# One cast and one subtraction of 2048 columns for the four sums of weights of a seven-product chunk, instead of two of each of 1024

## The chip, the core and the metric

One of the eight cores of a Trainium2 chip runs the kernel. The metric is device time in microseconds (us): the median of three runs. Each core has five engines that run their own instruction streams and wait for each other by semaphores: TensorE (PE in the profile, its weight loads PEld), VectorE (DVE), ScalarE (ACT), GpSimd (POOL) and SyncE (SP, which issues the DMAs here).

## What is computed

A decoder layer on 256 tokens of width 2048, all in float32:

```python
h = h + 0.5 * swiglu(rmsnorm(h, g_ffn1), w1_gate, w1_up, w1_down)   # D_FF = 5632
z = rmsnorm(h, g_mix) @ w_in
...                                                                # gating group A, windowed attention group B
h = h + y @ w_out
h = h + cross_attention(rmsnorm(h, g_x), rmsnorm(mem, g_mem), w_xq, w_xkv, w_xo)
h = h + 0.5 * swiglu(rmsnorm(h, g_ffn2), w2_gate, w2_up, w2_down)
return rmsnorm(h, g_final)
```

with `swiglu(x, wg, wu, wd) = (silu(x @ wg) * (x @ wu)) @ wd`. Almost all of the time goes into products of 256 rows with large weight matrices; the two SwiGLUs hold most of them.

## The kernel before

**Split products.** PE multiplies in the type fp32r. So that the result is good to float32, each operand is split into a high part (a cast, on ACT) and a low part (operand minus high part, on DVE), and each product is made in three passes: high by high, low activations by high weights, high activations by low weights. `split` does this: its cast is L146, its subtraction L147.

**Chunks and units.** The weights come in chunks of 1 MB (128 x 4 x 512). Eight chunks make a unit in the gate and up products (`gu_unit`; 11 units in each SwiGLU, named f1g and f2g in the profile); the down projections (f1d, f2d) have 44 chunks each, in four units. A chunk multiplies 2 x 2 blocks of activations by 2 x 2 blocks of weights in one of three ways: as eight plain products (N, C; 24 matmuls) or in a seven-product scheme (S; 21 matmuls). In an S chunk the seven products need sums of weight blocks, T1, T3, T2, T4 in this order: `load` (L304) adds them up into the tile t with three additions on DVE (L319 of 1024 columns, L322 and L323 of 512), splits three of the four raw blocks into wh and wl (1536 columns, L324), and then splits the four sums: two of them into one pair of tiles (th0, tl0), two into another (th1, tl1), in the loop at L326. In N and C chunks the four raw blocks are split at once into wh and wl (2048 columns). Units 2 to 9 of a gate and up product have kinds SCSCSCSC, units 0, 1 and 10 CCSCSCSC (unit 0 of the first SwiGLU is plain). 137 chunks are S chunks: 38 in f1g, 41 in f2g, 16 in f1d, 16 in f2d, 26 in the layer's middle.

**Buffers.** Raw weights have three buffers, wh and wl two each, t, th and tl one each. So the split of chunk n+2 into wh waits until PE is done with chunk n, and a th tile is written again only when PE has used the last one.

**Order on PE.** PE's order is written by hand. Matmuls are issued in `Unit.run` at L410. In the first and the last chunk of a unit the low weights of a product come right behind its high weights (`by_bank` in `passes`); in the chunks between, the low weights tl of the four sums come at the chunk's end (the list `behind`). Between matmuls, PE makes transposes of finished activations (L230, in `rows_done`, two groups for each unit, during chunk 2 of the next unit). Such a group needs a free bank of a ring of four in PSUM, which the unit's late products share; the second group gets its bank only when ACT has copied the first out (L665).

**Order on the other engines.** The instructions on DVE, ACT and SP are put in an order at build time by a scheduler with an idea of its own about how long each takes. On the chip, each engine runs its list strictly in that order. At the end of a unit the seven products are put together: `seven_early` behind the last S chunk (L560 to L562: p1, v and z), `seven_late` behind chunk 7 (L567 to L571), and then `gated` (an activation at L671, products at L675).

Of the kernel before, what the change touches and what calls it, by code (L numbers as in the profile page):

```python
# [9 lines left out]
F32R = mybir.dt.float32r  # L10
# [4 lines left out]
P = 128  # L15
# [17 lines left out]
def layer_kernel(  # L33
# [26 lines left out]
    stream = ctx.enter_context(tc.tile_pool(name="stream", bufs=2))  # L60
# [9 lines left out]
    def nm(s):  # L70
        uid[0] += 1
        return f"{s}_{uid[0]}"
# [72 lines left out]
    def split(hi, lo, src):  # L145
        nc.scalar.copy(hi, src)  # L146
        nc.vector.tensor_tensor(lo, src, hi.bitcast(F32), ALU.subtract)  # L147
# [162 lines left out]
    def load(s, w, kind, pieces, between):  # L310

        raw = stream.tile([P, 4, 512], F32, tag="raw", name=nm(s + "w"), bufs=3)
        wh = stream.tile([P, 4, 512], F32R, tag="wh", name=nm(s + "wh"))
        wl = stream.tile([P, 4, 512], F32R, tag="wl", name=nm(s + "wl"))
        b = {name: (wh[:, i, :], wl[:, i, :]) for name, i in SLOT.items()}
        if kind == "S":
            nc.sync.dma_start(raw, w)
            t = stream.tile([P, 4, 512], F32, tag="t", name=nm(s + "t"), bufs=1)
            nc.vector.tensor_tensor(  # L319
                t[:, 0:2, :], raw[:, 1:3, :], raw[:, 0:1, :].to_broadcast([P, 2, 512]), ALU.add  # L320
            )
            nc.vector.tensor_tensor(t[:, 2, :], t[:, 0, :], raw[:, 2, :], ALU.add)  # L322
            nc.vector.tensor_tensor(t[:, 3, :], t[:, 2, :], raw[:, 3, :], ALU.add)  # L323
            split(wh[:, 1:, :], wl[:, 1:, :], raw[:, 1:, :])  # L324

            for i, names in enumerate((("T1", "T3"), ("T2", "T4"))):  # L326
                th, tl = [
                    stream.tile([P, 2, 512], F32R, tag=f"{n}{i}", name=nm(s + n), bufs=1)
                    for n in ("th", "tl")
                ]  # L330
                split(th, tl, t[:, 2 * i:2 * i + 2, :])
                for j, name in enumerate(names):
                    b[name] = th[:, j, :], tl[:, j, :]
        elif pieces:
            for n, i in enumerate(pieces):
                between(n)
                nc.sync.dma_start(raw[:, i, :], w[:, i, :])
                split(wh[:, i, :], wl[:, i, :], raw[:, i, :])
        else:
            nc.sync.dma_start(raw, w)  # L340
            split(wh, wl, raw)
        return b
# [133 lines left out]
    def push(u, i, w, p, post=None, pieces=None, beside=None, before=None, ending=None):  # L476
        if before is not None and i:
            before(i)
        b = load(u.s, w, u.kinds[i], pieces, lambda n: before(i, n) if i == 0 else None)
        if beside is not None:  # L480
            beside(i)

        def run():
            first, last = [f("S") if "S" in u.kinds else -1 for f in (u.kinds.find, u.kinds.rfind)]
            if u.late and all(name in u.left for name in u.late):
                held[0] = first <= i <= last

                ends[0] = now[0] + 2 if u.clear and i == first - 1 else None
            held[0] = held[0] or i in u.alone
            tight[0] = u.sparse and first <= i <= last  # L490
            if ending is None:
                u.multiply(u.kinds[i], p(), b, i in (0, len(u.kinds) - 1))
            elif not u.kept:
                u.kept.append((p(), b))
            else:
                u.multiply_two(u.kept[0], (p(), b), ending)
            held[0] = False
            ends[0] = None

        turn(run, post)  # L500
# [980 lines left out]
```

## Time and profile before

| What | Value |
| --- | --- |
| median of 3 runs | 2049.44 us (2048.94 to 2049.57) |
| span of the profiled execution, first to last instruction | 2047.2 us |
| PE busy | 2034.8 us (99%) |
| DVE busy | 1859.5 us (91%), 1998 instructions |
| ACT busy | 1225.4 us (60%), 1344 instructions |
| mean granted TensorE clock | 0.999 |
| DMA | 402.21 MB, mean 196 GB/s |

The profiled execution's own time is known only as its span; the runs are timed from outside it, and their median is 2.2 us above the span. In rows of groups, a tile's name stands without its number: f1gtl is a tl of the first gate and up product, f1gP and f1gQ are banks in which products add up, f1a holds transposed activations, n1fh the high part of the activations. A row gives the operation, output and inputs, shape, count, the busy time and the mean of one in ns, and the idle time before it by what ended it. In rows of the timeline the first number is the start in us, the second the duration, and a bracket at the end the idle time before and its releaser.

### The profile page before, as it was taken

The numbers are of one execution on the slowest core, as the hardware profiler recorded it, in microseconds if no ns is written. First come the engines' busy times: TensorE is split into PE (matmuls) and PEld (weight loads), VectorE is DVE, ScalarE is ACT, GpSimd is POOL, SyncE is SP. The second block draws the span as 40 slices with busy tenths as digits, with TensorE's granted clock in tenths as the row PEclk, the third lists the DMA queues.
The fourth block names the chain that finished last, engine by engine and source line by source line (L and its number), as shares of the span: only waits on it lengthen the run. The fifth ranks groups of instructions, "written<-read, shape, count | busy, mean of one in ns | idle before, by whom it ended". The sixth has DMA issues, their size and how long they took to land.

```text
span 2047.2 us, 24505 instructions
## 1 busy us (share of the span) xinstructions
PE 2034.8 (99%) x9411; PEld 1690.0 (83%) x9411; DVE 1859.5 (91%) x1998; ACT 1225.4 (60%) x1344; POOL 36.6 (2%) x57
## 2 busy tenths in 40 slices
PE   9999999999999999999999999999999999999998
PEld 7888888888888888888888888888888888888886
DVE  6999999999998978988988977899999999999988
ACT  7755555565555766655556665675555556565554
POOL 0000000000000110100000000000000000000000
PEclk9999999999999999999999999999999999999999
DMA  8555555555555565545545544455455555555563
GB/s 312 182 207 204 206 206 185 205 209 192 203 204 203 188 241 178 195 162 185 202 169 186 204 150 155 171 195 214 185 206 202 205 193 206 202 203 209 185 224 126
DMA packets 60421, 402.21 MB, mean 196 GB/s; under 512 B 6912, under 2 KB 8976, under 8 KB 13200
## 3 DMA queue, kind: packets, MB, share of 16 engines
q1 hardware_dynamic: 57856, 393.50, 53.0%
q0 software_dynamic: 2016, 6.30, 0.9%
q8 instruction: 74, 1.21, 0.2%
q10 hardware_dynamic: 432, 0.84, 0.1%
q14 instruction: 43, 0.35, 0.1%
HBM read 398.52 MB, written 2.10 MB: 196 GB/s over the span
## 4 chain that ended last, share of the span: by engine, by line
PE 97%; DVE 1%; ACT 1%; issue 0%; DMA 0%; POOL 0%; POOLq 0%; DVEq 0%; SPq 0%
PE f1gQ L410 16%; PE f2gQ L410 15%; PE f2dQ L410 6%; PE f1dQ L410 6%; PE f1gP L410 6%; PE f2gP L410 6%; PE xqQ L410 3%; PE f2dP L410 3%; PE f1dP L410 3%; PE woQ L410 2%; PE xoQ L410 2%; PE f2dR L410 2%; PE f1dR L410 2%; PE vQ L410 2%; PE mv0Q L410 2%; PE mv1Q L410 2%
## 5 line engine op out<-in xcount | busy, mean ns | idle before, releaser
L147 DVE TENSOR_TENSOR f1gwl<-f1gw,f1gwh 128x1536 fp32r<-128x1536 f32 (+2 forms) x94 | 181.7, 1935 | 19.8 <-ACT f1gwh L146 16.0
L146 ACT CAST f2gwh<-f2gw 128x1536 fp32r<-128x1536 f32 (+1 forms) x88 | 150.7, 1712 | 69.0 <-PE f2gQ L410 45.5
L146 ACT CAST f1gwh<-f1gw 128x1536 fp32r<-128x1536 f32 (+2 forms) x94 | 153.0, 1629 | 59.9 <-PE f1gQ L410 39.0
L147 DVE TENSOR_TENSOR f2gwl<-f2gw,f2gwh 128x1536 fp32r<-128x1536 f32 (+1 forms) x88 | 179.4, 2039 | 9.5 <-ACT f2gwh L146 7.8
L146 ACT CAST f2gth<-f2gt 128x1024 fp32r<-128x1024 f32 x82 | 84.9, 1050 | 75.9 <-DVE f2gt L319 28.8
L146 ACT CAST f1gth<-f1gt 128x1024 fp32r<-128x1024 f32 x76 | 79.0, 1051 | 76.1 <-DVE f1gt L319 30.1
L410 PE MATMUL f2gQ<-f2gwh,n4fh 128*128 128x512 f32 x317 | 124.5, 393 | 0.0
L410 PE MATMUL f2gQ<-f2gwh,n4fl 128*128 128x512 f32 x317 | 123.4, 389 | 0.0
L146 ACT CAST f2dwh<-f2dw 128x2048 fp32r<-128x2048 f32 (+1 forms) x44 | 77.3, 1757 | 61.6 <-PE f2dQ L410 39.6
L410 PE MATMUL f1gQ<-f1gwh,n1fh 128*128 128x512 f32 x286 | 112.4, 393 | 0.0
L410 PE MATMUL f1gQ<-f1gwh,n1fl 128*128 128x512 f32 x286 | 111.3, 389 | 0.0
L146 ACT CAST f1dwh<-f1dw 128x2048 fp32r<-128x2048 f32 (+1 forms) x44 | 77.3, 1758 | 56.6 <-PE f1dQ L410 38.1
L147 DVE TENSOR_TENSOR f2gtl<-f2gt,f2gth 128x1024 fp32r<-128x1024 f32 x82 | 99.6, 1220 | 8.9 <-ACT f2gth L146 8.4
L147 DVE TENSOR_TENSOR f1dwl<-f1dw,f1dwh 128x2048 fp32r<-128x2048 f32 (+1 forms) x44 | 92.1, 2093 | 12.6 <-ACT f1dwh L146 12.5
L147 DVE TENSOR_TENSOR f2dwl<-f2dw,f2dwh 128x2048 fp32r<-128x2048 f32 (+1 forms) x44 | 92.1, 2094 | 11.5 <-ACT f2dwh L146 11.3
L147 DVE TENSOR_TENSOR f1gtl<-f1gt,f1gth 128x1024 fp32r<-128x1024 f32 x76 | 92.4, 1220 | 7.7 <-ACT f1gth L146 7.2
L410 PE MATMUL f2gQ<-f2gwl,n4fh 128*128 128x512 f32 x317 | 97.6, 392 | 0.0
L410 PE MATMUL f1gQ<-f1gwl,n1fh 128*128 128x512 f32 x286 | 88.0, 393 | 0.0
L410 PEld LDWEIGHTS f2gQ<-f2gwh,n4fh 128*128 128x128 f32 x317 | 59.5, 188 | 12.3 <-DVE f2gv L569 0.4
L410 PEld LDWEIGHTS f2gQ<-f2gwh,n4fl 128*128 128x128 f32 x317 | 59.5, 188 | 11.9
L410 PE MATMUL f2gP<-f2gwh,n4fh 128*128 128x512 f32 x176 | 68.8, 391 | 0.0
L410 PEld LDWEIGHTS f2gQ<-f2gwl,n4fh 128*128 128x128 f32 x317 | 58.8, 188 | 12.0
(828 smaller groups left out, 6045.8 us busy)
## 6 DMA issues: line engine op xcount, KB each, us to landing
f2gw<-in_w_gu SPq DMA_DIRECT2D x88, 1024.0 KB, 4.8
f1gw<-in_w_gu SPq DMA_DIRECT2D x86, 1024.0 KB, 4.9
f1dw<-in_w_down SPq DMA_DIRECT2D x44, 1024.0 KB, 4.8
f2dw<-in_w_down SPq DMA_DIRECT2D x44, 1024.0 KB, 4.8
wow<-in_w_out SPq DMA_DIRECT2D x16, 1024.0 KB, 4.8
xqw<-in_w_xq SPq DMA_DIRECT2D x16, 1024.0 KB, 4.8
xow<-in_w_xo SPq DMA_DIRECT2D x16, 1024.0 KB, 4.8
qw<-in_w_in SPq DMA_DIRECT2D x8, 1024.0 KB, 4.8
```

Source lines behind the costliest of these rows:

```text
L146: nc.scalar.copy(hi, src)
L147: nc.vector.tensor_tensor(lo, src, hi.bitcast(F32), ALU.subtract)
L410: nc.tensor.matmul(self.banks[name], x, y, start=name not in self.begun, stop=self.left[name] == 0)
```

## The change

The loop of two splits of 1024 columns becomes one split of 2048 columns, into one th and one tl tile of four blocks. The sums are in t in the order in which the loop took them. The footprint of the buffers is the same: two tiles of 1024 columns before, one of 2048 now.

```diff
@@ -323,14 +323,12 @@
             nc.vector.tensor_tensor(t[:, 3, :], t[:, 2, :], raw[:, 3, :], ALU.add)
             split(wh[:, 1:, :], wl[:, 1:, :], raw[:, 1:, :])
 
-            for i, names in enumerate((("T1", "T3"), ("T2", "T4"))):
-                th, tl = [
-                    stream.tile([P, 2, 512], F32R, tag=f"{n}{i}", name=nm(s + n), bufs=1)
-                    for n in ("th", "tl")
-                ]
-                split(th, tl, t[:, 2 * i:2 * i + 2, :])
-                for j, name in enumerate(names):
-                    b[name] = th[:, j, :], tl[:, j, :]
+            th, tl = [
+                stream.tile([P, 4, 512], F32R, tag=n, name=nm(s + n), bufs=1) for n in ("th", "tl")
+            ]
+            split(th, tl, t)
+            for j, name in enumerate(("T1", "T3", "T2", "T4")):
+                b[name] = th[:, j, :], tl[:, j, :]
         elif pieces:
             for n, i in enumerate(pieces):
                 between(n)
```

In each S chunk one cast and one subtraction go, and the others have twice the columns: 137 instructions fewer on ACT and 137 fewer on DVE. The lists of PE, SP and POOL are the same as before, those of DVE and ACT are in another order. Three places are shown here. In the rows, a number behind a name tells tiles of one name apart, and lines behind L330 have numbers lower by 2 in the new kernel.

Place 1 is chunk 2 of unit 7 in the first gate and up product. On DVE before, f1gt_2556, f1gwl_2554 and f1gtl_2563 and f1gtl_2567 belong to chunk 2, f1gwl_2602 to chunk 3:

```order
L319 TENSOR_TENSOR f1gt_2556<-f1gw_2552 128x1024
L147 TENSOR_TENSOR f1gwl_2554<-f1gw_2552,f1gwh_2553 128x1536
L322 TENSOR_TENSOR f1gt_2556<-f1gt_2556,f1gw_2552 128x512
L147 TENSOR_TENSOR f1gtl_2563<-f1gt_2556,f1gth_2562 128x1024
L323 TENSOR_TENSOR f1gt_2556<-f1gt_2556,f1gw_2552 128x512
L147 TENSOR_TENSOR f1gwl_2602<-f1gw_2600,f1gwh_2601 128x2048
L147 TENSOR_TENSOR f1gtl_2567<-f1gt_2556,f1gth_2566 128x1024
```

The subtraction for chunk 3 (f1gwl_2602) stood between the two halves of tl. On DVE now, with f1gtl_2467 of chunk 2 and f1gwl_2502 of chunk 3:

```order
L319 TENSOR_TENSOR f1gt_2460<-f1gw_2456 128x1024
L147 TENSOR_TENSOR f1gwl_2458<-f1gw_2456,f1gwh_2457 128x1536
L322 TENSOR_TENSOR f1gt_2460<-f1gt_2460,f1gw_2456 128x512
L323 TENSOR_TENSOR f1gt_2460<-f1gt_2460,f1gw_2456 128x512
L147 TENSOR_TENSOR f1gwl_2502<-f1gw_2500,f1gwh_2501 128x2048
L147 TENSOR_TENSOR f1gtl_2467<-f1gt_2460,f1gth_2466 128x2048
L147 TENSOR_TENSOR f1gwl_2535<-f1gw_2533,f1gwh_2534 128x1536
```

The subtraction for chunk 3 now stands ahead of the whole tl of chunk 2. On ACT at the same place before, with f1gwh_2601 of chunk 3:

```order
L146 CAST f1gwh_2553<-f1gw_2552 128x1536
L146 CAST f1gth_2562<-f1gt_2556 128x1024
L146 CAST f1gwh_2601<-f1gw_2600 128x2048
L665 COPY f1a_2517<-f1a_2588 128x512
L146 CAST f1gth_2566<-f1gt_2556 128x1024
L665 COPY f1a_2517<-f1a_2612 128x512
L146 CAST f1gwh_2634<-f1gw_2633 128x1536
```

The first copy of f1a stood ahead of the second half of th. On ACT now, with f1gwh_2501 of chunk 3:

```order
L146 CAST f1gwh_2457<-f1gw_2456 128x1536
L146 CAST f1gwh_2501<-f1gw_2500 128x2048
L146 CAST f1gth_2466<-f1gt_2460 128x2048
L663 COPY f1a_2421<-f1a_2488 128x512
L663 COPY f1a_2421<-f1a_2512 128x512
L146 CAST f1gwh_2534<-f1gw_2533 128x1536
```

Both copies now stand behind the whole th of chunk 2.

Place 2 is the boundary from unit 7 to unit 8 of that product. On DVE before, f1gwl_2746 belongs to chunk 7 of unit 7, f1gwl_2779 and the tiles f1gtl to chunk 0 of unit 8, and f1gv, f1gp, f1gz and f1u to the end of unit 7:

```order
L147 TENSOR_TENSOR f1gwl_2746<-f1gw_2744,f1gwh_2745 128x2048
L323 TENSOR_TENSOR f1gt_2781<-f1gt_2781,f1gw_2777 128x512
L147 TENSOR_TENSOR f1gwl_2779<-f1gw_2777,f1gwh_2778 128x1536
L561 TENSOR_TENSOR f1gv_2772<-f1gQ_481_2529,f1gp_518_2771 128x512
L147 TENSOR_TENSOR f1gtl_2788<-f1gt_2781,f1gth_2787 128x1024
L567 TENSOR_TENSOR f1gp_518_2771<-f1gP_477_2525,f1gp_518_2771 128x512
L562 TENSOR_TENSOR f1gz_2773<-f1gQ_480_2528,f1gv_2772 128x512
L147 TENSOR_TENSOR f1gtl_2792<-f1gt_2781,f1gth_2791 128x1024
L568 TENSOR_TENSOR f1u_2819<-f1gQ_479_2527,f1gz_2773 128x512
L569 TENSOR_TENSOR f1gv_2772<-f1gQ_479_2527,f1gv_2772 128x512
L571 TENSOR_TENSOR f1gz_2773<-f1gQ_482_2530,f1gz_2773 128x512
L570 TENSOR_TENSOR f1gv_2772<-f1gQ_478_2526,f1gv_2772 128x512
```

The low parts of chunk 0 stood among the first steps of the unit's end. On DVE now, with f1gwl_2638 of chunk 7, f1gwl_2671 and f1gtl_2680 of chunk 0:

```order
L559 TENSOR_TENSOR f1gv_2664<-f1gQ_433_2433,f1gp_464_2663 128x512
L322 TENSOR_TENSOR f1gt_2673<-f1gt_2673,f1gw_2669 128x512
L565 TENSOR_TENSOR f1gp_464_2663<-f1gP_429_2429,f1gp_464_2663 128x512
L560 TENSOR_TENSOR f1gz_2665<-f1gQ_432_2432,f1gv_2664 128x512
L323 TENSOR_TENSOR f1gt_2673<-f1gt_2673,f1gw_2669 128x512
L566 TENSOR_TENSOR f1u_2707<-f1gQ_431_2431,f1gz_2665 128x512
L567 TENSOR_TENSOR f1gv_2664<-f1gQ_431_2431,f1gv_2664 128x512
L147 TENSOR_TENSOR f1gwl_2671<-f1gw_2669,f1gwh_2670 128x1536
L568 TENSOR_TENSOR f1gv_2664<-f1gQ_430_2430,f1gv_2664 128x512
L569 TENSOR_TENSOR f1gz_2665<-f1gQ_434_2434,f1gz_2665 128x512
L673 TENSOR_TENSOR f1gp_464_2663<-f1gv_2664,f1gp_464_2663 128x512
L147 TENSOR_TENSOR f1gtl_2680<-f1gt_2673,f1gth_2679 128x2048
```

The subtraction f1gwl_2638 stands two rows ahead of the first row shown, and the addition L319 between them. The low part wl of chunk 0 now stands behind seven steps of 512 columns (v, the two additions, p, z, u, v), and tl behind three more and wl.

Place 3 is chunk 10 of the first down projection. On DVE before, with f1dwl_4192 of chunk 11:

```order
L147 TENSOR_TENSOR f1dwl_4150<-f1dw_4148,f1dwh_4149 128x1536
L322 TENSOR_TENSOR f1dt_4152<-f1dt_4152,f1dw_4148 128x512
L147 TENSOR_TENSOR f1dtl_4159<-f1dt_4152,f1dth_4158 128x1024
L323 TENSOR_TENSOR f1dt_4152<-f1dt_4152,f1dw_4148 128x512
L208 TENSOR_TENSOR f1af_4200<-f1a_1893 128x256
L147 TENSOR_TENSOR f1dwl_4192<-f1dw_4190,f1dwh_4191 128x2048
L147 TENSOR_TENSOR f1dtl_4163<-f1dt_4152,f1dth_4162 128x1024
```

Only the second half of tl stood behind the next chunk's wl. On DVE now, with f1dwl_4024 of chunk 11:

```order
L319 TENSOR_TENSOR f1dt_3988<-f1dw_3984 128x1024
L147 TENSOR_TENSOR f1dwl_3986<-f1dw_3984,f1dwh_3985 128x1536
L322 TENSOR_TENSOR f1dt_3988<-f1dt_3988,f1dw_3984 128x512
L208 TENSOR_TENSOR f1af_4032<-f1a_1829 128x256
L323 TENSOR_TENSOR f1dt_3988<-f1dt_3988,f1dw_3984 128x512
L213 TENSOR_TENSOR f1af_4032<-f1a_1829,f1af_4032 128x128
L208 TENSOR_TENSOR f1af_4183<-f1a_2125 128x256
L214 TENSOR_TENSOR f1af_4032<-f1a_1829,f1af_4032 128x128
L147 TENSOR_TENSOR f1dwl_4024<-f1dw_4022,f1dwh_4023 128x2048
L147 TENSOR_TENSOR f1dtl_3995<-f1dt_3988,f1dth_3994 128x2048
```

The whole tl stands behind it, and four short steps for the activations (f1af) stand ahead. The order of place 1 on DVE is found in chunk 2 of all units 2 to 9 of both gate and up products; in all but one of these 16 (unit 2 of the second) the copies stand behind th as well. The order of place 2 is found at the boundaries into units 2 to 9 of the first and 3 to 9 of the second product. The order of place 3 is found in 6 chunks of each down projection (chunks 4, 10, 12, 14, 26 and 28 of 44).

## The prediction

> **What bounds the kernel now.** I read the page first: busy times, then the chain that ended last.
>
> ```profile
> span 2047.2 us, 24505 instructions
> PE 2034.8 (99%) x9411; PEld 1690.0 (83%) x9411; DVE 1859.5 (91%) x1998; ACT 1225.4 (60%) x1344; POOL 36.6 (2%) x57
> PE 97%; DVE 1%; ACT 1%; issue 0%; DMA 0%; POOL 0%; POOLq 0%; DVEq 0%; SPq 0%
> ```
>
> PE is busy for all but 12.4 us and makes 97% of the chain. DVE has 9% left over the whole span. So time can be won from what PE waits for, which is next to nothing; time can be lost wherever DVE or ACT deliver later than PE wants. Next the waits of PE's weight loads, of which these two bear on the change, and the stretch of unit 7 of the first gate and up product (columns: stretch, length, busy time of PE, PEld, DVE, ACT, POOL, granted clock, DMA share, GB/s):
>
> ```profile
> PEld xoQ L410 <- ACT n4r L248: 1.6, 1, 1.6
> PEld f1gQ L410 <- DVE f1gtl L147: 0.4, 1, 0.4
> 305.60:347.30 41.70, 41.70 (x189) 34.53 (x188) 39.98 (x38) 24.15 (x21) 0.00 (x0) 1.00 0.55 202
> ```
>
> One wait in the whole program is for a tl in f1g, 0.4 us. But in such a unit DVE works 39.98 of 41.70 us: it keeps up with 4% to spare, and its order decides what is in time.
>
> **What the engines save.** The rows of the split by shape, for f1g:
>
> ```profile
> L147 DVE TENSOR_TENSOR f1gwl<-f1gw,f1gwh 128x2048 fp32r<-128x2048 f32 x48 | 109.8, 2288 | 16.9 <-ACT f1gwh L146 13.0 <-PE f1gQ L410 3.1 <-PE f1gP L410 0.6
> L147 DVE TENSOR_TENSOR f1gtl<-f1gt,f1gth 128x1024 fp32r<-128x1024 f32 x76 | 92.4, 1220 | 7.7 <-ACT f1gth L146 7.2
> ```
>
> A subtraction of 2048 columns (as wl in C chunks has today) takes 2.29 us, two of 1024 take 2.44: by durations 0.15 us less. But operations overlap. In this piece of DVE's timeline (end of unit 7) the starts tell what each really holds the engine for:
>
> ```profile
> 338.50 2.29 DVE L147 TENSOR_TENSOR f1gwl<-f1gw,f1gwh 128x2048 fp32r<-128x2048 f32 x1
> 340.70 0.69 DVE L323 TENSOR_TENSOR f1gt<-f1gt,f1gw 128x512 f32<-128x512 f32 x1
> 341.30 1.75 DVE L147 TENSOR_TENSOR f1gwl<-f1gw,f1gwh 128x1536 fp32r<-128x1536 f32 x1
> 342.97 0.68 DVE L561 TENSOR_TENSOR f1gv<-f1gQ,f1gp 128x512 f32<-128x512 f32 x1
> 343.57 1.21 DVE L147 TENSOR_TENSOR f1gtl<-f1gt,f1gth 128x1024 fp32r<-128x1024 f32 x1
> 344.71 0.68 DVE L567 TENSOR_TENSOR f1gp<-f1gP,f1gp 128x512 f32<-128x512 f32 x1
> 345.90 1.21 DVE L147 TENSOR_TENSOR f1gtl<-f1gt,f1gth 128x1024 fp32r<-128x1024 f32 x1
> ```
>
> Start to start: 2048 columns 2.20 us, 1536 columns 1.67, 1024 columns 1.14, 512 columns 0.60. So one subtraction instead of two saves 2 x 1.14 - 2.20 = 0.08 us, over 137 S chunks about 11 us of DVE, which isn't the bound: worth nothing by itself. The Trainium skill, "VectorE: DVE Perf Modes", section on the TRN2 errata, puts the fixed cost of an operation at about 150 cycles and lets a large tile pay it once; an estimate from it, 0.16 us at 0.96 GHz, agrees with the difference of the durations (0.15), but the starts show half of it hidden. By the page's figure DVE would be 0.08 us earlier for each S chunk, and the boundary sum below, with two whole tl in its chain, some 2 us less over 14 boundaries.
>
> The ACT row is read below: a cast of 2048 columns takes 1.91 us, two of 1024 take 2 x 1.05 less an overlap of about 0.09. That is 0.1 us a chunk on an engine that is 60% busy: nothing.
>
> **What moves, place 1: the copies behind the whole th (chunk 2 of units 2 to 9).** The timeline of before in unit 7, a chunk-3 wh first:
>
> ```profile
> 314.43 1.91 ACT L146 CAST f1gwh<-f1gw 128x2048 fp32r<-128x2048 f32 x1 [0.86 <-PE f1gQ L410]
> 316.25 0.58 ACT L665 COPY f1a<-f1a 128x512 f32<-128x512 f32 x1
> 316.72 1.06 ACT L146 CAST f1gth<-f1gt 128x1024 fp32r<-128x1024 f32 x1
> 316.72 2.29 DVE L147 TENSOR_TENSOR f1gwl<-f1gw,f1gwh 128x2048 fp32r<-128x2048 f32 x1 [0.31 <-ACT f1gwh L146]
> 317.62 0.14 PEld L230 LDWEIGHTS f1a<-ident,f1gp 128*128 128x128 f32 x1
> 318.49 0.59 ACT L665 COPY f1a<-f1a 128x512 f32<-128x512 f32 x1 [0.71 <-PE f1a L230]
> 318.93 1.22 DVE L147 TENSOR_TENSOR f1gtl<-f1gt,f1gth 128x1024 fp32r<-128x1024 f32 x1
> 318.99 1.48 ACT L146 CAST f1gwh<-f1gw 128x1536 fp32r<-128x1536 f32 x1
> 320.60 0.87 PEld L410 LDWEIGHTS f1gQ<-f1gtl,n1fh 128*128 128x128 f32 x4
> ```
>
> Today the first copy of f1a runs 316.25 to 316.83, and the second group of transposes, which needs the bank that it empties, begins at 317.62: 0.8 us to spare. Now ACT makes wh (until 316.34), then the whole th from 316.25 to 318.16, then the copy from 318.07 to 318.65. The transposes can begin at about 318.70, so PE waits 318.70 - 317.62 = 1.08 us. On DVE the whole tl starts where its second half does now, 318.93, and ends 318.93 + 2.29 = 321.22; its first use, 320.60, has moved to 321.68 by the wait before, so there is no second one. Fifteen such chunks x 1.08, and unit 2 of f2g, where the copies stay ahead and tl alone is late by 321.22 - 320.60 = 0.62: **17 us**. The cost lies on PE, which has no slack to take it up.
>
> **Place 2: the boundary into the next unit.** The second copy now ends at 318.49 + 1.08 + 0.59 = 320.16, wh of chunk 4 runs 320.07 to 321.55, and from there DVE's list is a chain. The latency from a finished sum to its cast is read here:
>
> ```profile
> 324.73 0.69 DVE L323 TENSOR_TENSOR f1gt<-f1gt,f1gw 128x512 f32<-128x512 f32 x1
> 325.53 1.05 ACT L146 CAST f1gth<-f1gt 128x1024 fp32r<-128x1024 f32 x1 [2.95 <-PE f1gQ L410]
> ```
>
> 0.11 us from 325.42. Today the first half of th is cast while DVE makes the last sum, and DVE subtracts the one half while ACT casts the other. Now tl stands right behind the last sum, and DVE idles for the cast: 0.11 + 1.91 + 0.03 = about 2.05 us, in chunk 4 and in chunk 6. By starts: wl of chunk 4 at 321.58, sums 323.25 to 325.68, th 325.79 to 327.70, tl 327.73, wl of chunk 5 329.93, the first sum (1.14) 332.13, wl of chunk 6 333.27, sums until 336.23, th until 338.25, tl 338.28, wl of chunk 7 340.48 (2 us later than the 338.50 above), the first sum of chunk 0 at 342.68, then seven steps of 0.60 from 343.82, wl of chunk 0 348.02 to 349.77, three more steps, tl 351.49 to 353.78. What PE wants, from the loads that begin unit 8:
>
> ```profile
> 347.35 0.19 PEld L410 LDWEIGHTS f1gP<-f1gwh,n1fh 128*128 128x128 f32 x1
> 347.80 0.19 PEld L410 LDWEIGHTS f1gP<-f1gwl,n1fh 128*128 128x128 f32 x1
> 349.84 0.19 PEld L410 LDWEIGHTS f1gQ<-f1gtl,n1fh 128*128 128x128 f32 x1
> ```
>
> With the 1.08 of place 1, wl is wanted at 348.88 and comes at about 349.80: 0.92 late. tl is then wanted at 349.84 + 1.08 + 0.92 = 351.84 and comes at 353.81: 1.97 late. Together 2.89 us. Before itself has one boundary with its tl so late, into unit 2:
>
> ```profile
> 98.83 0.19 PEld L410 LDWEIGHTS f1gQ<-f1gtl,n1fh 128*128 128x128 f32 x1
> 99.32 1.22 DVE L147 TENSOR_TENSOR f1gtl<-f1gt,f1gth 128x1024 fp32r<-128x1024 f32 x1
> 100.59 0.19 PEld L410 LDWEIGHTS f1gQ<-f1gtl,n1fh 128*128 128x128 f32 x1 [0.44 <-DVE f1gtl L147]
> ```
>
> There the second half ends at 100.54, and PE waits 0.44 for it, the one wait for tl listed above. With the whole tl there the first use at 98.83 waits too, until 100.54: about 1.7, 1.3 more than today. Into units 3 to 9 of f1g and of f2g, 14 x 2.89 = 40.5; with 1.3, **42 us**. From below, if DVE gets to the boundary no later than today, nothing; from above, each further microsecond on the chain costs 14 us. I take the chain, since every step of it has a row.
>
> **Place 3: the down projections.** Chunk 10 of the first, before:
>
> ```profile
> 525.34 1.92 ACT L146 CAST f1dwh<-f1dw 128x2048 fp32r<-128x2048 f32 x1 [1.46 <-issue]
> 527.31 2.29 DVE L147 TENSOR_TENSOR f1dwl<-f1dw,f1dwh 128x2048 fp32r<-128x2048 f32 x1
> 529.51 1.22 DVE L147 TENSOR_TENSOR f1dtl<-f1dt,f1dth 128x1024 fp32r<-128x1024 f32 x1
> 530.54 0.87 PEld L410 LDWEIGHTS f1dQ<-f1dtl,f1afh 128*128 128x128 f32 x4
> ```
>
> Only the second half of tl stands behind the next chunk's wl, and it ends at 530.73, after the first use of tl but before its own. Now the whole tl does: 527.31 + 2.20 + 2.29 = 531.80 against 530.54, 1.26 us of waiting. Twelve such chunks: **15 us**. wl can't come earlier, as it waits for its wh (525.34 + 1.92 = 527.26). In chunks 4 and 6 of a unit I cost the later tl at nothing: by the chain it ends at 330.0 and 340.6, and its first use, the chunk's 18th matmul, comes at 332.1 and 342.0 (0.22 us a matmul, from 41.70 us for 189 in the row above, 135 matmuls and 8 transposes ahead of chunk 6, 90 and 8 ahead of chunk 4, 17 within each, and 1.08 from place 1). That is a cover of 2.1 and 1.4 us; a chain later than that costs there too. One more chunk, at the start of f2g, has the order of place 1 on DVE; I take 0.5.
>
> **Sum.** 17 + 42 + 15 + 0.5 = 74.5 us, against the profiled span of 2047.2: 2121.7. The median of the runs lies 2.2 above that span: **2124 us**.
>
> **Rivals.**
> *Only the waits inside chunks.* DVE has 1.7 us to spare in a unit of 41.7, and each wait of PE gives it more; if the chain of place 2 reaches the boundary as early as today, only places 1 and 3 cost: 2049.4 + 17 + 15 = 2082. For it: each wait gives ACT and DVE time to get ahead. Against: they get ahead only as far as the buffers let them, and the two idle stretches of 2.05 us stand in the list.
> *A longer chain.* If the chain is 2 us longer (each step after a wait adds a tenth or two, and raw weights may come later), 14 x 2 = 28 us more: 2152. Against: steps were taken from starts, with their latencies.
> *The clock falls.* In the row of a wait of 1.6 us,
>
> ```profile
> 1318.00:1324.00 6.00, 4.83 (x21) 3.66 (x21) 6.00 (x9) 5.12 (x11) 0.00 (x0) 1.00 0.22 59
> ```
>
> the granted clock stays 1.00. If waits of 0.9 and 2 us close together were enough to lower it, a stretch of 3.4 us at half the speed at each of 14 boundaries would add 24 us or more: 2148 and above. The Trainium skill, "TensorE: Matmul & The Clock Gate", Part 1, has the clock halved after an idle window of about 3.4 us; the waits here stay under that, so by that rule it holds.
> *Not slower.* The lists bind nowhere: the bank for the second transposes is free without the copy, and tl is ready by its first use because DVE, 0.08 us a chunk ahead, runs wl and tl sooner. Then the waits for f1gtl and its like go, 0.4 to 1.5 us in all, and the time is 2048 to 2049. It decides at place 1 if the transposes don't need the copy, and at place 3 if wl starts 1.26 us earlier. Against: wl starts 0.05 us behind its cast today.
>
> **How the numbers follow.** The forecast 0.70, only the waits inside chunks 0.12, a longer chain 0.10, the clock 0.03, not slower 0.05. The range takes in the forecast and the first rival: 2078 to 2146; the others, 0.18, are left out. What a measurement here can tell from no change is 0.2%, 4 us. Faster 0.01, same 0.04, slower 0.95.
>
> **What would show it.** In the waits of PEld: transposes f1a and f2a on the copies L663, 7 to 8 times each at 1.08 us; f1gwl and f1gtl at the boundaries, 0.9 and 2.0 us, 7 to 8 times each, and the same for f2g; f1dtl and f2dtl, 6 times each, 1.26. DVE's idle before L147 of tl should show 2 us after th in chunks 4 and 6. Unit 7 should last 41.7 + 1.1 + 2.9 us. The forecast is wrong if the time is under 2078, if PE's waits are for other tiles, or if the granted clock falls below 0.99.

## The result and the profile after

The changed kernel takes 2132.85 us (median of 4 runs, 2131.17 to 2133.26), the kernel before 2049.51 us beside it: a ratio of 1.0405 (95% interval 1.0392 to 1.0418), 83 us slower. 2124 us was forecast, with 2078 to 2146 as the range. The page of the changed kernel, the lines that answer to those of before:

```profile
span 2129.4 us, 24046 instructions
PE 2055.5 (97%) x9411; PEld 1685.6 (79%) x9411; DVE 1852.6 (87%) x1861; ACT 1205.6 (57%) x1207; POOL 36.1 (2%) x57
PE 66%; DVE 17%; ACT 9%; issue 7%; ACTq 0%; DVEq 0%; POOL 0%; POOLq 0%
```

DVE has 6.9 us less work and ACT 19.8 us less, as the change means to, and the span is 82.2 us longer. The chain, 97% PE before, now goes through DVE and ACT for a quarter of the span. (PE's busy time grew by 20.7 us with the same 9411 matmuls; its ends are modelled, and time in which a matmul is held counts partly as busy.) The waits of PE's weight loads (total us, times, longest):

```profile
PEld f1gQ L408 <- DVE f1gtl L147: 16.8, 9, 2.1
PEld f2gQ L408 <- DVE f2gtl L147: 16.5, 9, 2.2
PEld f1gP L408 <- DVE f1gwl L147: 11.6, 9, 1.6
PEld f2gP L408 <- DVE f2gwl L147: 9.9, 7, 1.6
PEld f1a L230 <- ACT f1a L663: 8.8, 8, 1.1
PEld f2a L230 <- ACT f2a L663: 7.7, 7, 1.1
PEld f1dQ L408 <- DVE f1dtl L147: 6.4, 6, 1.3
PEld f2dQ L408 <- DVE f2dtl L147: 6.3, 6, 1.2
PEld xoQ L408 <- ACT n4r L248: 2.5, 2, 2.3
PEld f1dQ L408 <- ACT f1dth L146: 2.3, 6, 0.4
PEld f2dQ L408 <- ACT f2dth L146: 2.3, 6, 0.4
PEld woQ L408 <- ACT n3r L248: 1.9, 1, 1.9
```

The first eight are the three places of the prediction, with counts at or near the forecast ones: the second group of transposes (f1a, f2a), wl and tl at the boundary, tl in the down projections. They are 84.0 us (a load's wait begins while the last matmuls still run, so PE itself stands a few tenths less each time). By stage, from the first weight load of each to that of the next, nearly all of the loss lies in the two SwiGLUs:

| Stage | before, us | changed, us | difference |
| --- | --- | --- | --- |
| f1g, gate and up | 467.3 | 501.2 | 33.9 |
| f1d, down | 231.4 | 238.6 | 7.2 |
| the layer's middle | 640.4 | 643.0 | 2.5 |
| f2g, gate and up | 463.4 | 494.8 | 31.4 |
| f2d, down, to the end | 238.6 | 245.7 | 7.1 |

The rows around unit 7 in the first product, PE's waits and then DVE's idle times:

```profile
328.69 0.19 PEld L408 LDWEIGHTS f1gP<-f1gwl,n1fh 128*128 128x128 f32 x1 [1.39 <-DVE f1gwl L147]
332.69 0.19 PEld L408 LDWEIGHTS f1gQ<-f1gtl,n1fh 128*128 128x128 f32 x1 [2.06 <-DVE f1gtl L147]
343.22 0.14 PEld L230 LDWEIGHTS f1a<-ident,f1gp 128*128 128x128 f32 x1 [1.10 <-ACT f1a L663]
```

```profile
341.26 2.29 DVE L147 TENSOR_TENSOR f1gwl<-f1gw,f1gwh 128x2048 fp32r<-128x2048 f32 x1 [1.68 <-PE f1gQ L408]
345.94 1.76 DVE L147 TENSOR_TENSOR f1gwl<-f1gw,f1gwh 128x1536 fp32r<-128x1536 f32 x1 [0.19 <-ACT f1gwh L146]
352.34 2.29 DVE L147 TENSOR_TENSOR f1gtl<-f1gt,f1gth 128x2048 fp32r<-128x2048 f32 x1 [2.05 <-ACT f1gth L146]
363.02 2.29 DVE L147 TENSOR_TENSOR f1gtl<-f1gt,f1gth 128x2048 fp32r<-128x2048 f32 x1 [2.05 <-ACT f1gth L146]
372.77 1.75 DVE L147 TENSOR_TENSOR f1gwl<-f1gw,f1gwh 128x1536 fp32r<-128x1536 f32 x1
```

The two idle stretches of 2.05 us before tl, in chunks 4 and 6, are there to the hundredth. The stretch between two boundaries, from that load of wl at 328.69 to the next (374.57), by engine:

```profile
328.69:374.60 45.91, 42.63 (x189) 34.37 (x189) 39.80 (x34) 23.41 (x18) 0.00 (x0) 1.00 0.53 183
```

DVE worked 39.80 us here and idled 1.68 + 0.19 + 2.05 + 2.05 = 5.97 us in the rows above: 45.77 of 45.91 us. So in a unit DVE has nothing left to give, and PE's waits of 1.4, 2.1 and 1.1 us are where PE meets that. But not all of it is DVE's doing: the 1.68 us are a wait for PE, which comes out of the boundary late and gives up a buffer late. The work and the waits for casts alone are 44.09 us, already more than the 41.77 that the unit took before; with the 1.68 the unit is a loop. The chain that ended last goes round it: PE from 332.69 to 338.90, ACT's wh, th, copy and next wh until 345.92, then DVE and its two waits for th until the boundary. By group, DVE's idle time before tl in the gate and up products, most of it for ACT's cast, is 16.6 us before (8.9 and 7.7) and 79.8 us now:

```profile
L147 DVE TENSOR_TENSOR f2gtl<-f2gt,f2gth 128x2048 fp32r<-128x2048 f32 x41 | 93.8, 2289 | 41.8 <-ACT f2gth L146 41.7
L147 DVE TENSOR_TENSOR f1gtl<-f1gt,f1gth 128x2048 fp32r<-128x2048 f32 x38 | 87.0, 2289 | 38.0 <-ACT f1gth L146 38.0
```

So there are two theories to tell apart. By the prediction's sum, three places each cost for themselves, through the order of the lists. By the other, the merged steps take away an overlap: with halves, DVE sums and subtracts while ACT casts, with wholes it stands still, and since it had 1.7 us to spare in a unit, what it idles beyond that comes back as PE's waiting, wherever the order lets it show.

### The profile page after: what moved, and what is told of

Read it like the earlier page. It is cut to its first block, busy times and chain, and to the rows that moved or that the text cites. A ratio compares the mean times of both kernels' runs of the same rounds, so it can differ in the third digit from the quotient of the medians.

```text
span 2129.4 us, 24046 instructions
## 1 busy us (share of the span) xinstructions
PE 2055.5 (97%) x9411; PEld 1685.6 (79%) x9411; DVE 1852.6 (87%) x1861; ACT 1205.6 (57%) x1207; POOL 36.1 (2%) x57
## 4 chain that ended last, share of the span: by engine, by line
PE 66%; DVE 17%; ACT 9%; issue 7%; ACTq 0%; DVEq 0%; POOL 0%; POOLq 0%
PE f1gQ L408 7%; PE f2gQ L408 6%; PE f2dQ L408 5%; PE f1dQ L408 5%; PE xqQ L408 3%; DVE f2gwl L147 3%; PE f2dP L408 2%; PE f1dP L408 2%; PE f1gP L408 2%; DVE f1gwl L147 2%; PE woQ L408 2%; ACT f1gth L146 2%; PE f2gP L408 2%; PE xoQ L408 2%; ACT f2gth L146 2%
## 5 line engine op out<-in xcount | busy, mean ns | idle before, releaser
L147 DVE TENSOR_TENSOR f2gwl<-f2gw,f2gwh 128x1536 fp32r<-128x1536 f32 (+1 forms) x88 | 179.1, 2037 | 13.5 <-PE f2gQ L408 10.6
L146 ACT CAST f2gth<-f2gt 128x2048 fp32r<-128x2048 f32 x41 | 78.4, 1911 | 105.0 <-DVE f2gt L323 99.7
L147 DVE TENSOR_TENSOR f2gtl<-f2gt,f2gth 128x2048 fp32r<-128x2048 f32 x41 | 93.8, 2289 | 41.8 <-ACT f2gth L146 41.7
L146 ACT CAST f1gth<-f1gt 128x2048 fp32r<-128x2048 f32 x38 | 72.6, 1911 | 93.4 <-DVE f1gt L323 93.4
L147 DVE TENSOR_TENSOR f1gtl<-f1gt,f1gth 128x2048 fp32r<-128x2048 f32 x38 | 87.0, 2289 | 38.0 <-ACT f1gth L146 38.0
L408 PE MATMUL f2gP<-f2gwl,n4fh 128*128 128x512 f32 x176 | 64.0, 394 | 6.9 <-DVE f2gwl L147 6.9
L408 PEld LDWEIGHTS f2gQ<-f2gwh,n4fh 128*128 128x128 f32 x317 | 59.5, 188 | 12.0
```

The costliest lines, as they stand in the source:

```text
L408: nc.tensor.matmul(self.banks[name], x, y, start=name not in self.begun, stop=self.left[name] == 0)
```

## The experiments

**One cast, two subtractions.**

```diff
-            split(th, tl, t)
+            nc.scalar.copy(th, t)
+            for i in range(2):
+                k = slice(2 * i, 2 * i + 2)
+                nc.vector.tensor_tensor(tl[:, k, :], t[:, k, :], th[:, k, :].bitcast(F32), ALU.subtract)
```

> One cast of 2048 columns, two subtractions of 1024. The lists of DVE and ACT are as in the changed kernel at all three places (copies behind the whole th, the next chunk's wl ahead of both halves of tl, wl of the next unit behind seven steps), and DVE still waits for the whole th. Theory (order, and the wait for the whole th): place 1 and the waits at the boundary stay, so 2125 to 2137 us, with f1a and f2a waiting 1.1 us each in 15 chunks. Rival (the long subtraction: PE waits for a tl of 2048 columns where half would do): PE's first half of tl comes 1.1 us sooner at 14 boundaries and 12 chunks of the down projections, so under 2110 us.

2124.58 us, ratio 1.0365 (1.035 to 1.038). It is just under the theory's range and far above the rival's: 8 us of 83 go; with two subtractions left, the one cast brings the rest. PE's waits are for the same tiles (f1gtl 13.2 us, f1gwl 12.7, f1a 7.7).

**Two casts, one subtraction.**

```diff
-            split(th, tl, t)
+            for i in range(2):
+                k = slice(2 * i, 2 * i + 2)
+                nc.scalar.copy(th[:, k, :], t[:, k, :])
+            nc.vector.tensor_tensor(tl, t, th.bitcast(F32), ALU.subtract)
```

> Two casts of 1024 columns, one subtraction of 2048. In the lists, place 1 is as in the changed kernel (copies behind both casts), place 3 nearly so; at the boundary wl of the next unit stands behind no step of the unit's end and tl behind seven instead of ten. DVE waits only for the second cast: about 1.2 us instead of 2.05 in chunks 4 and 6. Theory: the boundary costs nothing or next to it, places 1 and 3 stay at 17 us each: 2078 to 2092 us. Rival (the long subtraction is what costs): 2120 us and more.

2097.68 us, ratio 1.0234 (1.0219 to 1.0249): between the two ranges, 6 us above the theory's, and 48 us slower than before. Of PE's waits:

```profile
PEld f1gQ L411 <- DVE f1gtl L332: 11.6, 9, 5.5
PEld f2gQ L411 <- DVE f2gtl L332: 7.9, 9, 2.3
PEld f2gQ L411 <- ACT f2gwh L146: 5.8, 7, 0.8
PEld f1a L230 <- ACT f1a L666: 1.4, 6, 0.2
```

At the boundary wl isn't waited for any more, as expected, but place 1 came out otherwise: with two casts, of which the first stands ahead of the next wh, the copies are in time (0.2 us), and what is waited for is tl and wh. DVE's idle time before tl is 41.3 us here (20.9 and 20.4 by its groups), between the 16.6 of before and the 79.8 of the change, and so is the time; the place is not what has the cost. The match is rough: 16.7 of the 41.3 us are for PE and only 24.6 for casts, and some 10 of the 48 us lie at one boundary, into unit 2 of f1g, where a single wait of 5.5 us stands and the clock falls behind it. In the steady units, 43.07 us long, DVE idles 1.12 us for a cast and 2.13 for PE.

**Down projections only.** Tiles of 2048 columns throughout, but the loop of halves outside f1d and f2d:

```diff
-            split(th, tl, t)
+            for k in (slice(0, 4),) if s in ("f1d", "f2d") else (slice(0, 2), slice(2, 4)):
+                split(th[:, k, :], tl[:, k, :], t[:, k, :])
```

> One cast and one subtraction only in the 32 seven-product chunks of the down projections, halves everywhere else, in tiles of 2048 columns throughout; elsewhere the lists are those of the kernel before. Theory: place 3 alone, 12 chunks with 1.0 to 1.4 us of waiting: 2062 to 2068 us, with no waits for tl in the gate and up products beyond those of before. Rival (tiles of 2048 columns cost by themselves, as PE's first use waits for both halves): waits in the gate and up products as well, 2080 us and more.

2064.61 us, ratio 1.0073 (1.0056 to 1.0089): 15.0 us, as the theory has it, 14.5 of them in the two down projections (7.2 and 7.3). The waits in the gate and up products are within a few tenths of before (f1g is 1.2 us longer, f2g 0.4), so the joint tiles cost next to nothing.

**The boundary in another order.** The changed kernel, and the five steps of `seven_late` put behind tl of the next unit's chunk 0, by an order that the build keeps on DVE and that makes no engine wait for another:

```diff
+    def behind_(second, first):
+        tc.add_manual_dep(second.ins, first.ins.name, ORDER_ONLY, reason="order")
...
-        nc.vector.tensor_tensor(dst(0, 0), u["P2"], p1, ALU.add)
+        late_(nc.vector.tensor_tensor(dst(0, 0), u["P2"], p1, ALU.add))
```

> The changed kernel with one more rule for the lists, which adds no wait between engines: the five steps that end a gate and up unit (p, u, v, v, z) stand behind tl of the next unit's chunk 0. Places 1 and 3 are as in the changed kernel. Theory (the boundary costs through its order, 54 us of waits): wl and tl of chunk 0 come in time or within 0.3 us, the unit's end comes some 4 us later than before the change; if the accumulation banks bear that, 2078 to 2090 us. Rival (the idle stretches of 2 us for the whole th make DVE late whatever the order): the boundary waits stay over 1.5 us each, 2100 us and more.

2144.28 us, ratio 1.0462 (1.0447 to 1.0478), slower than the change itself. The theory falls. The rival has the time right, though not the tiles. Of PE's waits, and then two stretches of two rows each:

```profile
PEld f1gP L422 <- DVE f1gp L579: 20.9, 8, 2.7
PEld f2gP L422 <- DVE f2gp L579: 20.4, 8, 2.7
PEld f1gQ L422 <- DVE f1gv L581: 5.3, 8, 0.7
PEld f2gQ L422 <- DVE f2gv L581: 5.3, 8, 0.7
```

```profile
191.23:194.64 3.41, 1.08 (x4) 0.49 (x3) 3.41 (x5) 1.83 (x2) 0.00 (x0) 1.00 0.94 310
194.64:198.05 3.41, 3.30 (x8) 2.62 (x9) 3.41 (x5) 2.00 (x2) 0.00 (x0) 0.50 0.00 0
283.38:286.79 3.41, 2.41 (x11) 1.67 (x9) 3.02 (x2) 3.41 (x2) 0.00 (x0) 1.00 0.41 115
286.79:290.20 3.41, 1.99 (x7) 1.31 (x8) 3.41 (x6) 0.91 (x3) 0.00 (x0) 1.00 0.53 221
```

wl and tl come in time at the boundary, as the order wants. But now PE waits for the banks that p and v empty: 41.3 us and 10.6, against 54.8 for wl and tl in the change. The order chose what is late; the lateness is the same. And here the granted clock (the third number from the end of a row) falls to 0.50 for 3.41 us behind 9 of the 16 boundaries with these waits: behind the wait of 2.63 us that ends at 193.55 it does, behind the same wait that ends at 287.99 it doesn't. Over the span the mean clock is 0.991 instead of 0.999. That accounts for the 11 us above the change: from the transposes of one unit to those of the next it is, but for the first such stretch, 47.0 to 47.3 us with a fall and 45.4 to 45.7 without, where the change has 45.9, so the nine falls cost some 14 us. Without them the run would be about as slow as the change, still far above the theory's range.

**wh behind the th before it.** The changed kernel, and on ACT the cast wh of a chunk of 2048 columns stands behind th of the chunk before:

```diff
-            split(th, tl, t)
+            last_t[0] = split(th, tl, t)
...
-            split(wh, wl, raw)
+            ws = split(wh, wl, raw)
+            if last_t[0] is not None:
+                behind_(ws[0], last_t[0][0])
+                last_t[0] = None
```

> The changed kernel with one rule for ACT's list, which adds no wait between engines: the cast wh of a chunk of 2048 columns stands behind the whole th of the seven-product chunk before it. In the lists, the first copy of f1a now stands right behind th and ahead of the next wh, and tl stands ahead of the next wl everywhere. Theory, mended by the last runs (in units 2 to 9 DVE itself is the bound: 39.8 us of work and the idle times before tl make the 45.9 us of such a unit): places 1 and 3 are gone, but chunk 2 now has an idle stretch of 2.05 us before its tl as chunks 4 and 6 have, in place of 1.68 us, so a unit stays near 46 us and the waits only move to the boundary: 2108 to 2122 us. Rival (each place costs by its order, and the sum of the places is the loss): places 1 and 3 are mended, 2095 to 2102 us.

2147.66 us, ratio 1.0484 (1.0468 to 1.05). The copies are not among the fifteen longest waits any more, places 1 and 3 are ordered as the prediction would wish, and the time is the longest of all. The rival is out by 46 us and the theory's range by 26: the theory had place 3 gone, but f1d and f2d take 239.7 and 248.3 us here, no less than in the change, and f2g takes 10 us more (504.9). DVE idles 2.05 us three times in a unit:

```profile
342.35 2.29 DVE L146 TENSOR_TENSOR f1gtl<-f1gt,f1gth 128x2048 fp32r<-128x2048 f32 x1 [2.05 <-ACT f1gth L146]
353.13 2.29 DVE L146 TENSOR_TENSOR f1gtl<-f1gt,f1gth 128x2048 fp32r<-128x2048 f32 x1 [2.05 <-ACT f1gth L146]
363.81 2.29 DVE L146 TENSOR_TENSOR f1gtl<-f1gt,f1gth 128x2048 fp32r<-128x2048 f32 x1 [2.05 <-ACT f1gth L146]
```

PE's waits have gathered at the boundary, in every second one as a single wait of about 3.5 us for wl:

```profile
147.31 0.29 PEld L417 LDWEIGHTS f1gP<-f1gwl,n1fh 128*128 128x128 f32 x1 [3.49 <-DVE f1gwl L146]
```

From this load to the one two units on (239.26) it is 91.95 us, or 46.0 a unit; in the change, from the load of wl at 328.69 to that of two units on (420.75), 92.06. So the unit's length in f1g is what it was, with all waits in another place. And here DVE waits for nothing but casts: 79.4 us of work and six times 2.05 make 91.7 of the 91.95. After the long waits the granted clock falls here too, ten times to 0.50 for 3.41 us (mean 0.991). In f2g, units with a fall last 46.7 to 47.0 us and units without 45.9, so the falls make a part of the 10 us there; the rest is open. PE loses at most 1.7 us of work in a fall, 17 us in ten: by that estimate the run would be at 2131 us or more without them, above both ranges all the same.

**The sums first.** The last kernel, and wl of a seven-product chunk put behind its three sums:

```diff
-            nc.vector.tensor_tensor(t[:, 3, :], t[:, 2, :], raw[:, 3, :], ALU.add)
-            split(wh[:, 1:, :], wl[:, 1:, :], raw[:, 1:, :])
+            sums = nc.vector.tensor_tensor(t[:, 3, :], t[:, 2, :], raw[:, 3, :], ALU.add)
+            behind_(split(wh[:, 1:, :], wl[:, 1:, :], raw[:, 1:, :])[1], sums)
```

> As the run with the cast ahead of the next chunk's, and one more rule for DVE's list, again without a wait between engines: in a seven-product chunk the low part wl of the raw blocks stands behind the three sums instead of ahead of the last two, so DVE has 1.67 us of work while ACT casts the whole th. Theory (the loss is DVE's idle time before tl): the idle stretch falls from 2.05 to some 0.4 us, a unit is back at PE's 41.7 us, 2046 to 2054 us, with one cast and one subtraction of 2048 columns in all 137 chunks. Rival (a subtraction and a cast of 2048 columns come too late by their length): boundary waits of 1 us and more stay, 2070 us and more.

2057.28 us, ratio 1.0037 (1.0025 to 1.005). 3 us above the theory's range, but 90 of the last run's 99 us are gone, with the same casts and subtractions of 2048 columns, no instruction added, and one rule of order for DVE as the only difference. A unit is back at 41.77 us. The rows show by what: wl covers the cast, and the idle time is 0.39.

```profile
328.32 1.75 DVE L146 TENSOR_TENSOR f1gwl<-f1gw,f1gwh 128x1536 fp32r<-128x1536 f32 x1
330.46 2.29 DVE L146 TENSOR_TENSOR f1gtl<-f1gt,f1gth 128x2048 fp32r<-128x2048 f32 x1 [0.39 <-ACT f1gth L146]
```

The waits at the boundaries and in the down projections are gone from the list. By stage, f1g is 5.6 us longer than before and the middle 3.7; the other three are within 0.3. What is left stands at single places:

```profile
PEld xoQ L417 <- ACT n4r L254: 2.5, 2, 2.3
PEld f1gQ L417 <- DVE f1gtl L146: 2.1, 1, 2.1
PEld woQ L417 <- ACT n3r L254: 1.9, 1, 1.9
PEld f1gQ L417 <- DVE n1fl L146: 1.8, 1, 1.8
PEld ya L236 <- issue: 1.5, 1, 1.5
```

**Down projections in order.** The kernel with the down projections only, and wh behind th in them:

```diff
+            whole = s in ("f1d", "f2d")
+            for k in (slice(0, 4),) if whole else (slice(0, 2), slice(2, 4)):
+                last_t[0] = split(th[:, k, :], tl[:, k, :], t[:, k, :])
+            if not whole:
+                last_t[0] = None
```

> One cast and one subtraction in the 32 seven-product chunks of the down projections alone, as in the run with the down projections only, and the rule that the next chunk's wh stands behind th, in the down projections only. Theory (place 3 is an effect of order: the next wl ahead of the whole tl): the 15 us are gone, 2047 to 2052 us, with no waits for f1dtl and f2dtl. Rival (the cast and the subtraction one behind the other, 1.91 + 2.29 us, are too long for the down projections in any order): waits for f1dtl stay, over 2055 us.

2065.45 us, ratio 1.0079 (1.0066 to 1.0091): no gain over the run without the rule. The theory falls: with tl ahead of the next wl, place 3 costs the same. Its waits only split up, in the first down projection 4.1 us for f1dth, 4.1 for f1dtl and 1.3 for f1dwl, and DVE idles 11.3 us before f1dtl, where it idled 0.1 before the change.

**Halves in order.** The kernel before, with wh and wl behind the last th and tl:

```diff
-                split(th, tl, t[:, 2 * i:2 * i + 2, :])
+                last_t[0] = split(th, tl, t[:, 2 * i:2 * i + 2, :])
...
+                behind_(ws[0], last_t[0][0])
+                behind_(ws[1], last_t[0][1])
```

> The kernel before, with its halves, and the rules that wh and wl of a chunk of 2048 columns stand behind th and tl of the seven-product chunk before it. Theory (with halves DVE never idles for a cast, and order at these places had slack): within 4 us of the kernel before, 2045 to 2053 us. Rival (the order with the next wl between the halves is what keeps DVE busy): DVE idles before the second half and the boundary waits come back, 2060 us and more.

2051.61 us, ratio 1.001 (1.0002 to 1.0019). The rule for wh that makes wholes 15 us slower than the change, here with one for wl besides, leaves halves within 0.2% of before.

**The copies first.** The changed kernel with the copies of f1a and f2a at high priority, which puts the first one ahead of the whole th, as before the change:

```diff
-                    nc.scalar.copy(a[:, q], ps)
+                    with tc.high_priority():
+                        nc.scalar.copy(a[:, q], ps)
```

> The changed kernel with the copies of f1a and f2a at high priority: on ACT the first copy of chunk 2 stands ahead of the whole th again, and DVE's list is as in the changed kernel at places 1 and 2. Rival (the prediction's sum: places 1 and 2 cost each for itself): 15 waits of 1.1 us go, less 0.6 us each for tl in chunk 2, so 2122 to 2127 us or less. Theory (DVE, with its idle time, is the bound of a unit; where PE waits within it is of no account): the copies' waits go, tl of chunk 2 and the boundary take their place, within 4 us of the changed kernel: 2129 to 2137 us, if the granted clock holds.

2129.46 us, ratio 1.0391 (1.0377 to 1.0406): 3.4 us less than the change, where the sum of places has 6 to 11. The waits for the copies are gone (16.5 us), and of tl:

```profile
PEld f1gQ L408 <- DVE f1gtl L147: 22.7, 16, 2.1
PEld f2gQ L408 <- DVE f2gtl L147: 21.4, 16, 2.2
```

There are 16 waits where there were 9 in each product, and 10.8 us more of them: chunk 2's tl is waited for now, some 0.77 us a time, where the rival had 0.6. So this run speaks for the theory only weakly: it lies 2.5 us above the rival's range and at the low end of the theory's.

**Halves made to wait.** The loop of halves, with two real waits that the wholes imply, the first cast for the last sum and the first subtraction for the second cast:

```diff
+            c0 = nc.scalar.copy(th[:, k0, :], t[:, k0, :])
+            wait_(c0, sums)
+            c1 = nc.scalar.copy(th[:, k1, :], t[:, k1, :])
+            d0 = nc.vector.tensor_tensor(tl[:, k0, :], t[:, k0, :], th[:, k0, :].bitcast(F32), ALU.subtract)
+            wait_(d0, c1)
+            nc.vector.tensor_tensor(tl[:, k1, :], t[:, k1, :], th[:, k1, :].bitcast(F32), ALU.subtract)
```

> Two casts and two subtractions of 1024 columns, as before, with two waits added that the whole steps imply: the first cast waits for the last sum, and the first subtraction for the second cast. Theory (the loss is the overlap of ACT's cast with DVE's sums and subtraction, not the merging of instructions, nor their length): 2120 to 2137 us, with idle stretches of some 2.1 us before tl in chunks 4 and 6. Rival (a long instruction is needed for the loss): 2050 to 2070 us.

2133.96 us, ratio 1.0413 (1.0399 to 1.0427), with no step longer than before: the whole loss, 84.7 us against 83.3. The idle stretches in chunks 4 and 6 of unit 7:

```profile
351.50 1.22 DVE L344 TENSOR_TENSOR f1gtl<-f1gt,f1gth 128x1024 fp32r<-128x1024 f32 x1 [2.14 <-ACT f1gth L343]
362.34 1.23 DVE L344 TENSOR_TENSOR f1gtl<-f1gt,f1gth 128x1024 fp32r<-128x1024 f32 x1 [2.15 <-ACT f1gth L343]
```

The build's order followed these waits, as it did the wholes (wl of the next chunk ahead of both halves, the copies behind both casts), so waits and order come together here. That wholes, or a changed order, cost little where no long idle stretch is left was seen with the sums first and with the halves in order; that another order which leaves the stretches in place doesn't mend the loss was seen at the boundary and with wh behind th.

**Wholes where they are covered.** Wholes with both rules in the gate and up units (from the end of unit 3 of f1g and from unit 3 of f2g on) and the down projections; halves elsewhere:

```diff
+            whole = s in ("f1d", "f2d") or s in ("f1g", "f2g") and loads[s] > 9
...
+            if whole:
+                behind_(low, sums)
```

> One cast and one subtraction, with the two rules of the run with the sums first, in the gate and up units from 2 on (chunks from 11 in the second) and in the down projections; halves without rules in the layer's middle and in the first units. Theory (the 8 us left with the sums first are single waits where ACT's longer cast stands ahead of the norms, at n1f, woQ and xoQ, and at the first boundary): they go, 2046 to 2053 us, the same as before, since DVE's saving buys nothing. Rival (the whole steps cost some tenths in every unit even with the sums first): 2055 us and more.

2050.95 us, ratio 1.0008 (0.9999 to 1.0017): no difference from before that could be told, with 91 subtractions fewer. The single waits of the run with the sums first that are listed above are gone but for xoQ at 1.6, which before has as well; in their stead PE waits once in each gate and up product for the step f1gv or f2gv of a unit's end (1.0 and 1.6 us). `loads` counts a product's seven-product chunks. DVE's busy time, 1860.3 us, isn't below the 1859.5 of before either, and PE is the bound again.

## Why the prediction was right, and where not

**Sign, size, places.** Right: 2132.85 against 2124 and the list of waits that was named, with counts of 6 to 9 where 6 to 8 were forecast. By stage, the gate and up products lost 65.3 us where 59.5 were set down, the down projections 14.3 where 15, and the middle 2.5 where nothing was. *What bounds the kernel* held: next to nothing to win at PE, and 1.7 us of DVE's to lose in a unit.

**What the engines save.** Of 11 us of DVE by starts, 6.9 were seen in its busy time in the change, and none in the run with the sums first (1860.9 us, all 137 subtractions fewer) or in the one with wholes where they are covered, which shows no gain from them. The Trainium skill's fixed cost ("VectorE: DVE Perf Modes", the section on the TRN2 errata) gives, as an estimate, some 21 us for 137 operations at 0.16 us; they were not seen in any of these.

**Place 1.** Forecast 1.08 us a time, 17 us in all; measured 1.10 and 16.5 for the copies, and 0.72 for the one tl in unit 2 of f2g (0.62 forecast). The one chunk at the start of f2g, set at 0.5, took 0.71.

**Place 2** was mis-sized: 0.92 for wl and 1.97 for tl forecast, 1.39 to 1.6 and 2.06 to 2.15 measured, so 3.5 us instead of 2.89, and 3.3 us into unit 2 of f1g, where 1.7 was forecast. 42 us were set down, some 53 came (54.8 in the four rows, less what has other causes). That is by the waits of weight loads, which overstate it: in length, a unit grew by 4.11 us (from 41.77 to 45.88, load of wl to load of wl), where places 1 and 2 had 3.97. Part of the chain's error can be read: a sum of 512 columns that reads the one just made starts 0.73 us behind it (348.87 to 349.60), not 0.60, and from wl of chunk 4 to wl of chunk 0 it is 26.83 us (345.94 to 372.77) where 26.44 were worked out.

```profile
348.87 0.69 DVE L322 TENSOR_TENSOR f1gt<-f1gt,f1gw 128x512 f32<-128x512 f32 x1
349.60 0.69 DVE L323 TENSOR_TENSOR f1gt<-f1gt,f1gw 128x512 f32<-128x512 f32 x1
```

**Place 3.** Forecast 15 us, measured 15.0 by itself and 14.3 in the change by stage. The waits for tl are the 12 that were worked out, of 1.1 us on average instead of 1.26, and another 12 of 0.4 us for th weren't forecast. But the order that was named isn't what the place costs: with tl ahead of the next wl, wholes cost the same 15 to 16 us there, so the right number doesn't bear out that reason. The down projections were back at their length of before only with the sums ahead of wl, which brings DVE's work under the cast.

**The sum of the places** is the weak step, though the number came out. 17 + 42 + 15 fits the change, but the places aren't costs of their own that could be taken off one by one. Removing the first gave 3.4 us, where the sum has 6 to 11; removing the lateness of wl and tl at the boundary by order gained nothing. The two idle stretches, which the prediction had in the chain of place 2 alone, are the cause throughout a unit: made on halves by two waits, with the order that followed these, they bring the whole loss; covered in wholes, 90 of 99 us go.

**The rivals.** *Only the waits inside chunks* named 2082 and was wrong for the reason given against it. *The clock falls* didn't come true in the change: the granted clock is 1.00 in 328.69 to 374.60, with waits of 1.4 and 2.1 us 4 us apart. It did in five of the experiments, behind waits of 2.3 to 5.5 us. *Not slower* needed tl in time, and it wasn't. Not foreseen were some single waits elsewhere, woQ at 1.9, xoQ 0.9 above before, n1fl at 1.3. They are gone where these parts keep their halves; which step makes them isn't shown.

## What to carry to other kernels

Where one engine makes a high part and another subtracts it, the number of pieces sets how much of the two overlaps; joining them saves little work on both and makes the second engine stand still for a whole cast, unless other work is put in between. Ask for each engine how much it has to spare in the stage, not over the span: 1.7 us in a unit against two new idle stretches of 2 us is enough to make the second-busiest engine the bound. Once that is so, an order that leaves the idle time in place only moves the wait; the idle time itself has to be covered, here by one rule that puts a subtraction behind three sums.

## What the runs showed of the hardware

The granted clock was more sensitive to waits than the row of before had led me to think (a wait of 1.6 us at clock 1.00), and the length of a wait alone doesn't settle it. In the changed kernel waits of up to 2.3 us left it at 1.00, the longest the 2.32 us for n4r at xoQ; in the runs with the boundary in another order and with wh behind th, the clock fell to 0.50 right behind that same wait of 2.32 us. In the five runs in which it fell while products ran, each fall lasted 3.41 us, or twice that behind the wait of 5.5 us in the run with one subtraction:

```profile
104.00:112.00 8.00, 5.28 (x12) 4.13 (x13) 6.85 (x6) 0.99 (x2) 0.00 (x0) 0.59 0.54 194
```

The falls of one run start whole multiples of 3.413 us apart: with the boundary in another order at 102.48, 194.64, 242.42, 334.58 and 382.37 in f1g, which is 27, 14, 27 and 14 such steps. By the profile, PE was busy at most 51% of the step ahead of each of the 24 falls, and at least 48% of every other step at full clock in these runs. That fits two equal waits with different outcomes: in the rows of the boundary run, the one that ends at 193.55 leaves PE 1.08 us of work in one step, the one that ends at 287.99 lies across two, with 2.41 and 1.99 us. PE's busy time is modelled, so the border near a half is rough.

The Trainium skill ("TensorE: Matmul & The Clock Gate", Part 1) has the clock halved after an idle window of about 3.4 us. The length agrees with the 3.41 us here, but the step ahead of a fall wasn't idle as a rule: PE was busy for 32% of the one at 191.23, and for up to 51% of others.
